# Two-layer hybrid encoder trunk: a room of their own for the gathered rows, one more buffer in the round of weight loads, and a smaller DMA scratch

## The chip, the cores and the metric

The kernel runs on one core of one Trainium2 chip. The metric is the device time of one execution in microseconds (us), shown as the median of several runs. The profile is one further execution, recorded by the hardware profiler; its instruction and DMA times are counted from the start of its span.

## The reference

512 tokens of width 1024 go through two layers and a last RMSNorm, all in float32. A layer is

```
h = rmsnorm(x); p = h @ w_in
o = concat[dilated-window heads | differential heads | latent heads]
x = x + o @ w_out
x = x + expert_choice_ffn(rmsnorm(x))

def expert_choice_ffn(h, ...):            # 16 experts, 64 tokens each
    affinity = softmax(h @ w_router)
    gate, idx = top_k(affinity^T, 64)     # every expert chooses its tokens
    xe = h[idx]                           # gather
    y = (silu(xe @ w_gate) * (xe @ w_up)) @ w_down * gate
    out[idx] += y                         # scatter and add
```

Each expert has three float32 matrices of 1024 x 1408 (w_gate, w_up) and 1408 x 1024 (w_down). All 16 experts of both layers are read once from HBM in each execution, about 554 MB.

## The kernel before, in words

**Phases.** In each layer an attention part (lines to about 880), then the router, which chooses the tokens, and then the expert part (lines 1098 to 1395), which the change is about. The attention part and the expert part use the same addresses of SBUF one after the other: their pools are opened and closed in turn, and a new tile waits until the last reader of whatever lay at its addresses is done.

**Pairs and steps.** The experts are taken two at a time: pair p = 0 to 7, one expert on each half of TensorE's columns. A pair has 24 steps of weights: 8 of the gate matrix, 8 of up, 8 of down. Step n (0 to 191 in a layer) is a block of 128 partitions x 2816 floats (1408 KB). So n = 0 to 7 is gate of pair 0, 8 to 15 up of pair 0, 16 to 23 down of pair 0, 24 to 31 gate of pair 1, 32 to 39 up of pair 1, and so on. Gate and up steps are the matmuls of line 1302, down steps those of line 1347. The order of the matmuls on TensorE is the order of the program.

**Loads.** `load(n)` issues the DMA of step n on the queue of SyncE (SP), in order of n; SP stands still at a load until its buffer is free, and with it everything behind it on that queue. Steps 0 to 16 are issued during the attention part in the order of the list `ISSUE`, each into a buffer as its place in SBUF comes free (line 1131, tiles `xslot`, `shared`, `apart`, `hx`). Steps 17 to 31 take the single buffers a second time in the order of the list `AGAIN` (line 1131, `xslot`). From step 32 on two steps come with one DMA of 2816 KB (line 1163, `dslot`) into one of seven double buffers, in the order of the string `DOUBLES`. Double buffer a lies where the single buffers x0 and x1 were, b where x2 and x3 were, and so on to f (x10, x11); g lies on y0 and y1. The last eight steps are issued one by one again.

**The list before.** With `AGAIN` = x0 to x9, y0, y1, x10, x11, x0, step 17 goes into x0, 18 into x1, ..., 26 into x9, 27 into y0 (free when step 11 is done), 28 into y1 (step 12), 29 into x10 (step 14), 30 into x11 (step 15), and 31 into x0 again (free when step 17 is done). With `DOUBLES` = bcdegfa, the steps 32 and 33 go into b (free when steps 19 and 20 are done), 34 into c (21, 22), 36 into d (23, 24), 38 into e (25, 26), 40 into g (27, 28), 42 into f (29, 30), 44 into a (31, 18).

**Marks and rows.** While pair p runs, pair p + 1 is prepared. At gate step `MARK_AT` = 6, `marks(p + 1)` builds the one-hot marks of the chosen tokens (line 1177), TensorE turns them into token numbers (line 1221) that VectorE copies into `slots` (lines 1225 to 1230), and turns the marks (lines 1236, 1239). `fetch_rows(p + 1)` then gathers the chosen 128 rows of x from HBM with one indirect DMA on GpSimd (POOL) (line 1248, 512 KB), and ScalarE (ACT) scales them (line 1249). After the up steps of pair p, ACT applies Silu to the gate sums (line 1327), VectorE (DVE) multiplies with the up sums (line 1328), `turn_rows` transposes the fetched rows for pair p + 1 (lines 1256, 1257), TensorE transposes the hidden values (line 1336), DVE copies them (line 1337), and the down steps begin (line 1347).

**Where the rows lie.** The rows of pairs 1 to 7 are put into the tile `shared`, tag `rows`, of 3072 floats. In the beginning of a layer's expert part this place holds the weights of step 10 (`(10, "rows")` in `ISSUE`). So the rows of pair 1 are fetched later than those of the others: after up step `ROWS_AT` = 2 of pair 0, which is step 10.

**Scratch.** `dynamic_dma_scratch_size` is the number of bytes of each SBUF partition that are set aside for the descriptors of the DMAs that POOL issues.

Of the kernel before, what the change touches and what calls it, by code (L numbers as in the profile page):

```python
# [11 lines left out]
F32 = mybir.dt.float32  # L12
# [10 lines left out]
P = 128  # L23
S = 512
D = 1024
# [4 lines left out]
FF = 1408  # L30
NJ = FF // P
CAP = 64
SLOT = 3072
RING = 3
ISSUE = [(16, "apart"), (0, "x0"), (1, "x1"), (4, "x4"), (11, "y0"), (2, "x2"), (3, "x3"), (10, "rows"), (5, "x5"), (6, "x6"), (7, "x7"), (9, "x9"), (8, "x8"), (13, "hx"), (14, "x10"), (15, "x11"), (12, "y1")]
AGAIN = ["x0", "x1", "x2", "x3", "x4", "x5", "x6", "x7", "x8", "x9", "y0", "y1", "x10", "x11", "x0"]
SINGLES = 32
DOUBLES = "bcdegfa"
GAP = 512
PAD = 168  # L40
AFTER = [[2, 3, 5, 8], [1, 5, 7, 10], [2, 3, 6, 9]]
# [20 lines left out]
ANGLES_FIRST = 26  # L62
EARLY = [[(0, 1)], [(1, 1)], [(2, 1)], [(3, 1)], []]
HALF_AT = 3
ROWS_AT = 2
END_ON = 'avavaa'
MARK_AT = 6
TAKE_UP = (3, 5)
# [72 lines left out]
def body(ctx, tc, x_in, x_t, pos, w_in, w_uq, w_ukv, w_out, w_gate, w_up, w_down, gatt, gfin, params, consts, band, sel, out):  # L141
    nc = tc.nc
# [7 lines left out]
    def nm(s):  # L150
        uid[0] += 1
        return f"{s}_{uid[0]}"
# [722 lines left out]
    for l in range(L):  # L875
        with ExitStack() as es:
# [218 lines left out]
            both = wide[:, :P].rearrange("p (t c e) -> p t c e", t=NT, c=2)  # L1095
            nc.vector.scalar_tensor_tensor(both, rank, 1.0, mask, op0=ALU.add, op1=ALU.mult)
            nc.vector.tensor_tensor(code, both[:, :, 0, :], both[:, :, 1, :], op=ALU.add)
        with tc.tile_pool(name=f"fs{l}", bufs=1, reuse_waits="tile") as fs, tc.tile_pool(name=f"fw{l}", bufs=2, side="right", reuse_waits="tile") as fw, ExitStack() as late:
            early = ExitStack()
            fx = early.enter_context(tc.tile_pool(name=f"fx{l}", bufs=1, reuse_waits="tile"))  # L1100
            streams = (w_gate, w_up, w_down)
# [1 line left out]
            def wide():  # L1103
                return fw.tile([P, 2 * FF], F32, tag="hx", bufs=1, name=nm("hx"))

            def shared():

                return fs.tile([P, SLOT], F32, tag="rows", name=nm("shared"))

            def single(tag):  # L1110
                return fx.tile([P, 2 * FF], F32, tag=tag, name=nm("xslot"))

            def source(n):

# [16 lines left out]
                    tc.keep_in_program_order(nc.sync.dma_start(v, src))  # L1131
                kept[n] = v

            near = {tag: single(tag) for tag in ("y0", "y1")}
            fx.tile([P, GAP], F32, tag="gap", name=nm("gap"))
            near.update({f"x{i}": single(f"x{i}") for i in range(12)})
            rooms = {}
            for n, tag in ISSUE:
                bring(n, xb.tile([P, 2 * FF], F32, tag="apart", name=nm("apart")) if tag == "apart" else wide() if tag == "hx" else shared()[:, : 2 * FF] if tag == "rows" else near[tag])

            def double(tag):
                return rooms["far"].tile([P, 4 * FF], F32, tag=tag, name=nm("dslot"))
# [1 line left out]
            def load(n):  # L1144

                if n not in kept:
                    if n < SINGLES:
                        bring(n, single(AGAIN[n - len(ISSUE)]))
                    else:
                        if n == SINGLES:  # L1150
                            early.close()
                            rooms["far"] = late.enter_context(tc.tile_pool(name=f"fd{l}", bufs=1, reuse_waits="tile"))
                            rooms["g"] = double("g")
                            rooms["far"].tile([P, GAP], F32, tag="gap", name=nm("gap"))
                            rooms.update({q: double(q) for q in "abcdef"})
                        tag = DOUBLES[(n - SINGLES) // 2 % len(DOUBLES)]
                        v = rooms.pop(tag) if tag in rooms else double(tag)
                        parts = [v[:, i * 2 * FF : (i + 1) * 2 * FF] for i in range(2)]
                        if n >= 23 * KD:
                            for i in range(2):  # L1160
                                bring(n + i, parts[i])
                        else:
                            tc.keep_in_program_order(nc.sync.dma_start(v, source(n)))
                            kept.update({n + i: parts[i] for i in range(2)})
                v = kept.pop(n)
                return v[:, :FF], v[:, FF:]
# [75 lines left out]
            def fetch_rows(p):  # L1242

                if p > 0:
                    v, src = shared()[:, :D], xrow_d[l][:, :]
                else:
                    v, src = fw.tile([P, S], F32R, tag="oh", bufs=3, name=nm("rows")).bitcast(F32), xrow_d[l].rearrange("t (h d) -> (t h) d", h=2)
                nc.gpsimd.indirect_dma_start(v, None, src, bass.IndirectOffsetOnAxis(token[:, p : p + 1], 0))  # L1248
                nc.scalar.activation(v, v, AF.Copy, scale=scales[:, p : p + 1])  # L1249
                return v  # L1250
# [41 lines left out]
            for p in range(8):  # L1292
                acc, whole = [], {}
                ahead = [] if p < 7 else [(t, h) for t in range(NT - 1) for h in range(2)] if l == L - 1 else [(t, h) for h in range(2) for t in range(NT)][:6]
                for s, w in enumerate((w_gate, w_up)):
                    bs = [bank() for _ in cuts]
                    acc.append(bs)
                    for k in range(KD):
                        ws = load((3 * p + s) * KD + k)
                        for b, (q0, qn) in zip(bs, cuts):  # L1300
                            for i in range(2):
                                tc.keep_in_program_order(nc.tensor.matmul(b[64 * i : 64 * i + 64, : qn * NJ], xe[:, k, 64 * i : 64 * i + 64], ws[i][:, q0 * NJ : (q0 + qn) * NJ], start=(k == 0), stop=(k == KD - 1)))  # L1302
                        if ahead and w is w_up and k in TAKE_UP:
                            take_x(*ahead.pop(0))
                        if w is w_gate and p == 0:
                            for f in EARLY[k + 1] if k + 1 < len(EARLY) else ():
                                fill(xg, xe, *f, pin=True)
                            if k == FIRST_MARKS:
                                numbers(first_oh, 0, pin=True)
                                rows = fetch_rows(0)  # L1310
                            if k == TURN_AT:
                                ohs[0] = turn_marks(first_oh, pin=True)
                            if k == HALF_AT:
                                turn_rows(rows, xe, 4, 4)
                        if w is w_gate and k in SCATTER_AT and pending is not None:
                            scatter(*pending, 2 * SCATTER_AT.index(k))
                        if w is w_gate and k == MARK_AT and p < 7:
                            ohs[p + 1] = marks(p + 1)
                            if p > 0:
                                rows = fetch_rows(p + 1)  # L1320
                        if w is w_up and k == ROWS_AT and p == 0:
                            rows = fetch_rows(1)
                hx = wide()
                hh, hT = hx[:, :FF].rearrange("p (j q) -> p j q", j=NJ), hx[:, FF:].rearrange("p (j s) -> p j s", j=NJ)
                for g, u, (q0, qn) in zip(acc[0], acc[1], cuts):
                    hv = hh[:, :, q0 : q0 + qn].rearrange("p j q -> p q j")
                    nc.scalar.activation(hv, g[:, : qn * NJ].rearrange("p (q j) -> p q j", j=NJ), AF.Silu)
                    nc.vector.tensor_tensor(hv, u[:, : qn * NJ].rearrange("p (q j) -> p q j", j=NJ), hv, op=ALU.mult)  # L1328
                if p < 7:
                    nxt = gathered()  # L1330
                    for k0 in (0, 4):
                        turn_rows(rows, nxt, k0)
                for j0, n in ((0, 4), (4, 4), (8, 3)):
                    b = bank()
                    for q in range(n):
                        nc.tensor.transpose(b[:, q * P : (q + 1) * P], hh[:, j0 + q, :], ident)
                    nc.vector.tensor_copy(hT[:, j0 : j0 + n, :], b[:, : n * P].rearrange("p (q s) -> p q s", q=n))
                bs = [bank(), bank()]
                for lo in range(0, NJ * D, FF):
                    hi = lo + FF  # L1340
                    ws = load((3 * p + 2) * KD + lo // FF)
                    e = lo
                    while e < hi:
                        j, h = e // D, e % D // 512
                        z = min(hi, (e // 512 + 1) * 512)
                        for i in range(2):
                            tc.keep_in_program_order(nc.tensor.matmul(bs[h][64 * i : 64 * i + 64, e % 512 : e % 512 + z - e], hT[:, j, 64 * i : 64 * i + 64], ws[i][:, e - lo : z - lo], start=(j == 0), stop=(j == NJ - 1)))  # L1347
                        e = z
                    if ahead and lo > FF:
                        take_x(*ahead.pop(0))  # L1350
                ys = results(p, bs)
                if p < 7:
                    pending = ohs.pop(p), ys
                    xe = nxt
# [133 lines left out]
```

## Time and profile before

| | |
|---|---|
| median of 3 runs | 1909.98 us (1909.73 to 1911.14) |
| the profiled execution's own time | 1910.87 us |
| its span | 1909.1 us |
| PE busy | 1722.2 us (90%), 8798 instructions |
| DVE, ACT, POOL busy | 703.6, 428.6, 206.1 us |
| read from HBM | 619.17 MB |
| DMA queue of SP and its share of 16 engines | 608.43 MB, 78.7% |
| DMAs issued by POOL (software queue) | 35.54 MB, 12128 packets, 7.9% |

The two expert parts are the stretches from about 325 to 950 us and from about 1267 to 1895 us. PE is TensorE's matmuls, PEld its weight loads; a "q" behind an engine's name is its sequencer, where DMAs are issued. PEclk is the granted clock of TensorE as a share of full speed. The time from issue to landing of a DMA holds the time that it spends behind other DMAs.

### The profile page before, as it was taken

The page shows a single profiled execution, that of the slowest core. Times are in us where ns is not written, and L with a number is a line of the kernel's source. Part 1 is how long each engine was busy: PE and PEld are TensorE (multiplying, and loading weights), DVE is VectorE, ACT ScalarE, POOL GpSimd, SP SyncE. Part 2 cuts the span into 40 slices and gives each one's busy share as a digit, 9 for nine tenths or more (in the row PEclk, how much of TensorE's full clock was granted, in tenths as well). Part 3 has the DMA queues.
Part 4 walks back from the last instruction along what each step waited for, and adds up shares of the span by engine and source line. Part 5 has one row for each costly group of instructions (what it writes and reads, how often), then busy time and mean ns, then how long its engine had stood idle before and what let it go on. Part 6 is the DMA issues. An engine that isn't in the chain of part 4 may idle for free.

```text
span 1909.1 us, 21766 instructions
## 1 busy us (share of the span) xinstructions
PE 1722.2 (90%) x8798; PEld 895.9 (47%) x8798; DVE 703.6 (37%) x1470; ACT 428.6 (22%) x884; POOL 206.1 (11%) x232
## 2 busy tenths in 40 slices
PE   8999999999987878888899999989998878888887
PEld 6785675344332333333377756743443333333333
DVE  7868856111211112111188698541121112111112
ACT  5347941101000100000043589211100100000101
POOL 1324421000000000000023153210000000000000
PEclk9999998999999999999999999989999999999999
DMA  7874649989999999999948744798999999999996
GB/s 274 248 199 72 163 149 365 396 351 429 429 428 431 428 430 429 429 428 429 397 131 267 170 101 110 246 363 352 409 429 428 430 429 429 429 429 428 430 427 264
DMA packets 82579, 649.28 MB, mean 340 GB/s; under 512 B 8656, under 2 KB 25808, under 8 KB 53040
## 3 DMA queue, kind: packets, MB, share of 16 engines
q1 hardware_dynamic: 68288, 608.43, 78.7%
q0 software_dynamic: 12128, 35.54, 7.9%
q10 hardware_dynamic: 2064, 3.93, 0.6%
q8 instruction: 69, 1.13, 0.2%
q14 instruction: 30, 0.25, 0.0%
HBM read 619.17 MB, written 27.39 MB: 339 GB/s over the span
## 4 chain that ended last, share of the span: by engine, by line
PE 48%; DMA 37%; DVE 9%; ACT 3%; issue 1%; POOL 1%; SPq 0%; DVEq 0%; ACTq 0%; POOLq 0%
PE ps L1302 16%; DMA dslot<-in_w_up_dram 13%; DMA dslot<-in_w_gate_dram 13%; DMA dslot<-in_w_down_dram 9%; PE ps L1347 7%; PE ps L753 6%; PE ps L854 5%; PE ps L762 2%; PE ps L672 2%; PE ps L1277 2%; PE ps L655 2%; DVE sm L604 1%; PE ps L515 1%; ACT P L611 1%; DMA shared<-xrow_d,slots 1%
## 5 line engine op out<-in xcount | busy, mean ns | idle before, releaser
L1302 PE MATMUL ps<-dslot,xe 128*64 128x506 f32 (+1 forms) x2496 | 528.7, 575 | 87.3 <-DMA dslot<-in_w_up_dram 51.7
L1302 PEld LDWEIGHTS ps<-dslot,xe 128*64 128x64 f32 x2496 | 178.3, 139 | 425.8 <-issue 321.3
L1347 PE MATMUL ps<-dslot,hx 128*64 128x512 f32 (+3 forms) x1568 | 275.8, 504 | 46.1 <-DMA dslot<-in_w_down_dram 41.6
L1347 PEld LDWEIGHTS ps<-dslot,hx 128*64 128x64 f32 x1568 | 104.5, 137 | 209.4 <-issue 136.9
L1328 DVE TENSOR_TENSOR hx<-ps,hx 128x506 f32<-128x506 f32 (+1 forms) x48 | 43.4, 968 | 428.7 <-PE ps L1302 383.7
L1269 DVE SCALAR_TENSOR_TENSOR hx<-ps,gates,hx 128x512 fp32r<-128x512 f32 x32 | 22.5, 746 | 363.3 <-ACT hx L1268 363.3
L1268 ACT ACTIVATE hx<-ps,gates 128x512 fp32r<-128x512 f32 x32 | 20.3, 684 | 605.1 <-PE ps L1347 605.1
L753 PE MATMUL ps<-xh,w 128*128 128x512 f32 (+1 forms) x448 | 145.8, 405 | 3.1 <-ACT xh L363 1.4
L1279 DVE TENSOR_TENSOR x<-ps,x 128x512 f32<-128x512 f32 x112 | 69.5, 683 | 184.1 <-PE ps L1277 184.1
L1249 ACT ACTIVATE shared<-shared,slots 128x1024 f32<-128x1024 f32 x14 | 16.1, 1148 | 488.5 <-DMA shared<-xrow_d,slots 455.3
L611 ACT ACTIVATE P<-ps,sm 128x512 f32<-128x512 f32 x168 | 116.5, 704 | 32.1 <-DVE sm L604 30.8
L1248 POOL DMA_INDIRECT shared<-xrow_d,slots x14 | 13.2, 943 | 945.6 <-DVE oh L1239 887.6
L1302 PE MATMUL ps<-xslot,xe 128*64 128x506 f32 (+1 forms) x528 | 109.4, 560 | 3.9 <-DVE xe L1208 2.3
L753 PEld LDWEIGHTS ps<-xh,w 128*128 128x128 f32 (+1 forms) x448 | 84.2, 189 | 28.0 <-ACT xh L363 3.9
L753 PE MATMUL ps<-xl,w 128*128 128x512 f32 (+1 forms) x224 | 85.7, 393 | 0.0
L604 DVE TENSOR_REDUCE sm<-ps 128x1 f32<-128x512 f32 x120 | 78.7, 679 | 5.5 <-PE ps L589 4.6
L655 PE MATMUL ps<-ident,P 128*128 128x128 f32 x512 | 77.5, 274 | 2.0 <-ACT P L611 1.8
L663 ACT COPY pt<-ps 128x512 f32<-128x512 f32 x118 | 68.9, 604 | 25.9 <-PE ps L655 25.9
L655 PEld LDWEIGHTS ps<-ident,P 128*128 128x128 f32 x512 | 62.1, 140 | 25.6 <-ACT P L611 7.4
L1302 PEld LDWEIGHTS ps<-xslot,xe 128*64 128x64 f32 x528 | 35.8, 136 | 67.4 <-issue 59.6
L762 PE MATMUL ps<-w,xh 128*128 128x320 f32 (+1 forms) x256 | 62.2, 326 | 2.3 <-DVE w L340 2.3
L340 DVE TENSOR_TENSOR w<-slot,w 128x1024 fp32r<-128x1024 f32 (+4 forms) x46 | 53.7, 1170 | 26.3 <-ACT w L339 23.4
(290 smaller groups left out, 2088.6 us busy)
## 6 DMA issues: line engine op xcount, KB each, us to landing
dslot<-in_w_up_dram SPq DMA_DIRECT2D x56, 2816.0 KB, 42.6
dslot<-in_w_down_dram SPq DMA_DIRECT2D x48, 2816.0 KB, 41.0
dslot<-in_w_gate_dram SPq DMA_DIRECT2D x48, 2816.0 KB, 41.8
xslot<-in_w_gate_dram SPq DMA_DIRECT2D x32, 1408.0 KB, 9.5
xslot<-in_w_down_dram SPq DMA_DIRECT2D x14, 1408.0 KB, 9.0
dslot<-in_w_down_dram SPq DMA_DIRECT2D x14, 1408.0 KB, 36.1
xslot<-in_w_up_dram SPq DMA_DIRECT2D x12, 1408.0 KB, 10.0
slot<-in_w_in_dram SPq DMA_DIRECT2D x8, 1536.0 KB, 9.6
```

What stands on the lines that cost most here:

```text
L340: rest = lambda o=o, m=m, src=src: nc.vector.tensor_tensor(w[:, 1, :, o : o + m], src, w[:, 0, :, o : o + m].bitcast(F32), op=ALU.subtract)
L604: nc.vector.tensor_reduce(mn, ps, axis=AX.X, op=ALU.min)
L611: nc.scalar.activation(e, ps, AF.Exp, bias=mn, scale=-1.0, accum_out=lcol)
L655: nc.tensor.transpose(b[:, kc * P : (kc + 1) * P], e[:, kc * P : (kc + 1) * P], ident)
L663: nc.scalar.copy(dv, bv)
L753: nc.tensor.matmul(b[:m], w[:, passes[j][0], k, :m], passes[j][1](k), start=(n == 0), stop=(n == 3 * KD - 1))
L762: nc.tensor.matmul(acc[t][:, :m], xs, w[:, c, kk, :], start=(k == 0 and j == 0), stop=(k == KD - 1 and j == 2))
L854: nc.tensor.matmul(blocks[t][1 + h], o, w[h], start=(i == 0), stop=(i == 3 * KD - 1))
L1279: nc.vector.tensor_tensor(xv, b, xv, op=ALU.add)
L1302: tc.keep_in_program_order(nc.tensor.matmul(b[64 * i : 64 * i + 64, : qn * NJ], xe[:, k, 64 * i : 64 * i + 64], ws[i][:, q0 * NJ : (q0 + q ...
L1328: nc.vector.tensor_tensor(hv, u[:, : qn * NJ].rearrange("p (q j) -> p q j", j=NJ), hv, op=ALU.mult)
L1347: tc.keep_in_program_order(nc.tensor.matmul(bs[h][64 * i : 64 * i + 64, e % 512 : e % 512 + z - e], hT[:, j, 64 * i : 64 * i + 64], ws[i][ ...
```

## The change

The rows of pairs 1 to 7 get a tile of 1024 floats in the pool `xb`, which is open through the whole kernel. The pool `fs` and its tile `shared` are gone. The place of 3072 floats becomes the single buffer `s` of the pool `fx`, with the same position in SBUF as before; step 10 is loaded into it as before, and it takes a second load in the round: `AGAIN` is now x0 to x9, s, y0, y1, x10, x11. `DOUBLES` is now abcdegf. From step 32 on the place of `s` stays empty. The rows of pair 1 are fetched together with its marks at gate step 6 of pair 0, as those of the other pairs are; `ROWS_AT` is gone. The scratch is 1024 bytes instead of 4096.

```diff
-ISSUE = [(16, "apart"), (0, "x0"), ..., (3, "x3"), (10, "rows"), (5, "x5"), ...]
-AGAIN = ["x0", "x1", "x2", "x3", "x4", "x5", "x6", "x7", "x8", "x9", "y0", "y1", "x10", "x11", "x0"]
+ISSUE = [(16, "apart"), (0, "x0"), ..., (3, "x3"), (10, "s"), (5, "x5"), ...]
+AGAIN = ["x0", "x1", "x2", "x3", "x4", "x5", "x6", "x7", "x8", "x9", "s", "y0", "y1", "x10", "x11"]
-DOUBLES = "bcdegfa"
+DOUBLES = "abcdegf"
-ROWS_AT = 2
...
-            def shared():
-                return fs.tile([P, SLOT], F32, tag="rows", name=nm("shared"))
             def single(tag):
-                return fx.tile([P, 2 * FF], F32, tag=tag, name=nm("xslot"))
+                return fx.tile([P, SLOT if tag == "s" else 2 * FF], F32, tag=tag, name=nm("xslot"))[:, : 2 * FF]
...
+            near = {"s": fx.tile([P, SLOT], F32, tag="s", name=nm("slot"))[:, : 2 * FF]}
+            near.update({tag: single(tag) for tag in ("y0", "y1")})
...
+                            rooms["far"].tile([P, SLOT], F32, tag="s", name=nm("lay"))
                             rooms["g"] = double("g")
...
                 if p > 0:
-                    v, src = shared()[:, :D], xrow_d[l][:, :]
+                    v, src = xb.tile([P, D], F32, tag="rows", name=nm("rows")), xrow_d[l][:, :]
...
                             ohs[p + 1] = marks(p + 1)
-                            if p > 0:
-                                rows = fetch_rows(p + 1)
-                        if w is w_up and k == ROWS_AT and p == 0:
-                            rows = fetch_rows(1)
+                            rows = fetch_rows(p + 1)
...
-    nc = _bacc.Bacc("TRN2", ..., dynamic_dma_scratch_size=4096)
+    nc = _bacc.Bacc("TRN2", ..., dynamic_dma_scratch_size=1024)
```

## Rows read from the trace of the kernel before

**Rows 1.** Chain of waits, 900 to 1000 and 1830 to 1910: start us, us, what

```profile
878.65 40.11 DMA dslot<-in_w_up_dram
...
1818.55 43.40 DMA dslot<-in_w_up_dram
```

**Rows 2.** By stretch: length, PE, PEld, DVE, ACT, POOL busy (xcount), PEclk, DMA share, GB/s

```profile
410.00:900.00 490.00, 424.02 (x2185) 170.54 (x2185) 86.92 (x152) 32.04 (x39) 6.22 (x7) 0.99 1.01 429
...
380.00:384.00 4.00, 4.00 (x14) 1.77 (x14) 1.61 (x3) 0.00 (x0) 0.00 (x0) 0.50 0.96 406
384.00:388.00 4.00, 4.00 (x28) 1.63 (x26) 0.00 (x0) 0.00 (x0) 0.00 (x0) 0.94 0.11 44
```

**Rows 3.** Timeline of SP: issues of steps 30, 32, 34; then layer 1's 30, 32

```profile
374.45 0.33 SPq L1131 DMA_DIRECT2D xslot<-in_w_gate_dram  x1
394.86 0.33 SPq L1163 DMA_DIRECT2D dslot<-in_w_up_dram  x1
399.60 0.33 SPq L1163 DMA_DIRECT2D dslot<-in_w_up_dram  x1
...
1316.38 0.33 SPq L1131 DMA_DIRECT2D xslot<-in_w_gate_dram  x1
1337.22 0.33 SPq L1163 DMA_DIRECT2D dslot<-in_w_up_dram  x1
```

**Rows 4.** DMA issues, us to landing: layer 0's 30 and 34, layer 1's 30, 32

```profile
xslot<-in_w_gate_dram SPq DMA_DIRECT2D x1, 1408.0 KB, 11.7
dslot<-in_w_up_dram SPq DMA_DIRECT2D x1, 2816.0 KB, 12.4
...
xslot<-in_w_gate_dram SPq DMA_DIRECT2D x1, 1408.0 KB, 12.4
dslot<-in_w_up_dram SPq DMA_DIRECT2D x1, 2816.0 KB, 9.9
```

**Rows 5.** Chain of waits, layer 0, end of the up steps of pair 0

```profile
362.88 9.30 DMA shared<-xrow_d,slots
...
373.50 1.28 ACT L1327
...
381.17 20.74 PE ps L1347 x112
```

**Rows 6.** Timeline, transposes of the rows at the end of pair 0, layer 0 and layer 1

```profile
374.34 1.10 PE L1256 MATMUL ps<-ident,shared 128*128 128x128 f32 x8
...
1316.27 1.10 PE L1256 MATMUL ps<-ident,shared 128*128 128x128 f32 x8
```

**Rows 7.** End of pair 1's up steps, layer 0: two of the timeline, one of the chain

```profile
444.35 2.72 DVE L1328 TENSOR_TENSOR hx<-ps,hx 128x506 f32<-128x506 f32 x3 [21.66 <-PE ps L1302]
445.68 1.09 PE L1256 MATMUL ps<-ident,shared 128*128 128x128 f32 x8
...
448.92 19.13 PE ps L1347 x112
```

**Rows 8.** Timeline, end of pair 1's marks; and pair 2's fetch, us to landing

```profile
353.02 0.69 DVE L1239 CAST oh<-ps 128x512 fp32r<-128x512 f32 x1
...
shared<-xrow_d,slots POOLq DMA_INDIRECT x1, 13.2
```

**Rows 9.** Timeline, layer boundary: first load of layer 1 on SP; first weight cast on ACT

```profile
931.53 0.34 SPq L322 DMA_DIRECT2D pg<-in_params_dram  x1
...
957.50 1.04 ACT L339 CAST w<-slot 128x1024 fp32r<-128x1024 f32 x1
```

**Rows 10.** POOL's densest DMAs; all of their kind, us to landing; packets of a row fetch

```profile
136.57 2.19 POOL L524 DMA_DIRECT2D st<-bst_d  x4 [21.32 <-PE ps L762]
139.12 2.15 POOL L524 DMA_DIRECT2D st<-bst_d  x4 [0.37 <-PE ps L528]
...
st<-bst_d POOLq DMA_DIRECT2D x40, 256.0 KB, 4.2
q0 software_dynamic: 144, 0.52, 11.8%
```

More of the change, by code (lines that the diff above doesn't have):

```diff
@@ L34 @@
 RING = 3
-ISSUE = [(16, "apart"), (0, "x0"), (1, "x1"), (4, "x4"), (11, "y0"), (2, "x2"), (3, "x3"), (10, "rows"), (5, "x5"), (6, "x6"), (7, "x7"), (9, "x9"), (8, "x8"), (13, "hx"), (14, "x10"), (15, "x11"), (12, "y1")]
-AGAIN = ["x0", "x1", "x2", "x3", "x4", "x5", "x6", "x7", "x8", "x9", "y0", "y1", "x10", "x11", "x0"]
+ISSUE = [(16, "apart"), (0, "x0"), (1, "x1"), (4, "x4"), (11, "y0"), (2, "x2"), (3, "x3"), (10, "s"), (5, "x5"), (6, "x6"), (7, "x7"), (9, "x9"), (8, "x8"), (13, "hx"), (14, "x10"), (15, "x11"), (12, "y1")]
+AGAIN = ["x0", "x1", "x2", "x3", "x4", "x5", "x6", "x7", "x8", "x9", "s", "y0", "y1", "x10", "x11"]
 SINGLES = 32
-DOUBLES = "bcdegfa"
+DOUBLES = "abcdegf"
 GAP = 512
@@ L1097, in body @@
             nc.vector.tensor_tensor(code, both[:, :, 0, :], both[:, :, 1, :], op=ALU.add)
-        with tc.tile_pool(name=f"fs{l}", bufs=1, reuse_waits="tile") as fs, tc.tile_pool(name=f"fw{l}", bufs=2, side="right", reuse_waits="tile") as fw, ExitStack() as late:
+        with tc.tile_pool(name=f"fw{l}", bufs=2, side="right", reuse_waits="tile") as fw, ExitStack() as late:
             early = ExitStack()
@@ L1132, in bring @@
                 kept[n] = v
-            near = {tag: single(tag) for tag in ("y0", "y1")}
+            near = {"s": fx.tile([P, SLOT], F32, tag="s", name=nm("slot"))[:, : 2 * FF]}
+            near.update({tag: single(tag) for tag in ("y0", "y1")})
             fx.tile([P, GAP], F32, tag="gap", name=nm("gap"))
@@ L1138, in body @@
             for n, tag in ISSUE:
-                bring(n, xb.tile([P, 2 * FF], F32, tag="apart", name=nm("apart")) if tag == "apart" else wide() if tag == "hx" else shared()[:, : 2 * FF] if tag == "rows" else near[tag])
+                bring(n, xb.tile([P, 2 * FF], F32, tag="apart", name=nm("apart")) if tag == "apart" else wide() if tag == "hx" else near[tag])
             def double(tag):
@@ L1474 @@
     from concourse.bass_utils import run_bass_kernel_spmd as _run
-    nc = _bacc.Bacc("TRN2", target_bir_lowering=False, num_devices=1, dynamic_dma_scratch_size=4096)
+    nc = _bacc.Bacc("TRN2", target_bir_lowering=False, num_devices=1, dynamic_dma_scratch_size=1024)
     arrays, args = {}, []
```

## The prediction

> **What bounds the kernel now.** I read the page's summary first (TensorE 90% busy, SP's queue 78.7% of the DMA engines), then the chain of waits, then the stretches, then the loads one by one. The reader should see three things.
>
> The expert part of a layer is a stream of weights. From 410 to 900 us the engines moved 429 GB/s at a DMA share of 1.01 [rows 2]: nothing more fits in. By that rate a step of 1408 KB takes 3.36 us and a double one 6.72 us. The last wait in each layer is for a load of the up matrix of pair 7: step 182 lands at 878.65 + 40.11 = 918.8 us, its like in layer 1 at 1818.55 + 43.40 = 1862.0 [rows 1]. Behind these landings stand only the last matmuls and the end of the layer. So a microsecond that the stream loses anywhere after it has filled up is paid at the end of the layer.
>
> It loses some at its beginning. From 384 to 388 us the share is 0.11 [rows 2]. Step 30 landed at 374.45 + 11.7 = 386.15 and step 34 at 399.60 + 12.4 = 412.0 [rows 3, 4]. Between lie 25.9 us, but the loads in them (31, then two doubles) are 3.36 + 2 x 6.72 = 16.8 us of work. **9.1 us** were lost. In layer 1 step 30 landed at 1316.38 + 12.4 = 1328.8 and step 32 at 1337.22 + 9.9 = 1347.1: 18.3 us for 10.1 us of work, **8.2 us** lost.
>
> The reason is in the order of the buffers. Step 31 waits in x0 until step 17 is done, step 32 in b until step 20 is done; both are down steps of pair 0. And these come late, for the rows of pair 1 could be fetched only at 362.88, when step 10 had left their place. They landed at 372.2; ACT then scaled them, loaded its table (1.28 us) and began Silu at 374.8 [rows 5], although TensorE had ended the up steps before 374.34, where it starts to transpose the rows [rows 6]. The down steps began at 381.17, and TensorE's clock had dropped: 0.50 granted from 380 to 384, that is its level of 1.2 GHz [rows 2].
>
> **The change, part by part.**
>
> *Rows with the marks.* The fetch goes out when the marks of pair 1 are done, 353.02 + 0.69 = 353.7 us [rows 8], in place of 362.88. It lands 9.3 us later [rows 5], or 13.2 as for pair 2 [rows 8]: at 363.0 to 366.9. Behind it on ACT wait the scaling (1.15 us), the table and three Silus (2.6); nothing else is due there. All are done at 368 to 372. DVE needs the first Silu where the last up sums end, by pair 1 1.33 us ahead of the rows' transposes (444.35 against 445.68 [rows 7]), so at 373.0. It fits, with 1 us to spare in the worse case. POOL has nothing behind this fetch before pair 2's. The fetch itself is 0.52 MB, 1.2 us of the stream, moved some 9 us ahead within it: the bytes stay the same, and the loads that it then delays are of down steps, which TensorE reaches after 377 us at the earliest, so this costs nothing (were the cover gone: 1.2 us a layer).
>
> Then the end of pair 0 looks like that of pair 1, where the down steps start 448.92 - 445.68 = 3.24 us after the transposes [rows 7]. Pair 0 would start them at 374.34 + 3.24 = 377.6, not 381.17, and run them in 19.13 us, not 20.74 [rows 5, 7], because the long idle time ahead of them is gone: 3.6 + 1.6 = 5.2 us earlier for TensorE at the end of pair 0. In layer 1: 1316.27 + 3.24 = 1319.5 [rows 6].
>
> *The eleventh step's buffer.* Steps 27 to 31 each take the buffer freed one load before, so step 31 is no longer tied to step 17: it may go out when step 15 is done, where step 30 goes out now (374.45), and lands right behind it, 386.15 + 3.36 = 389.5 (layer 1: 1332.1). Step 32 now waits for step 18 in a, not 20 in b. A down step takes 19.13 / 8 = 2.39 us, so step 18 is done at 377.6 + 3 x 2.39 = 384.8 (layer 1: 1326.7). A load into an empty stream has its first bytes after about 9.9 - 6.72 = 3.2 us [rows 4]: 388.0, ahead of 389.5 (layer 1: 1329.9 ahead of 1332.1). The stream does not stop. Step 34 (b, free after step 20 at 389.5) needs to flow at 396.2, 36 (after 22 at 394.3) at 403, and the distance grows by 6.72 - 4.8 us for each double. So both losses go in full: 9.1 + 8.2 = **17.3 us**. Unknown here: whether the gap closes wholly; I take it so, with 0 to 4 us left open, since the margins are 1.5 and 2.2 us.
>
> TensorE does not need these loads at once, and its own 5.2 us are not added: the landing at 918.8 decides, and it moves by the stream's gain. What is late next is again that landing, 9.1 us earlier.
>
> *The names in the round.* The double buffers still come round after seven, so the wait between a load and its buffer is the same from step 46 on. But a and g are each last used one double step later. In layer 1's beginning SP waits for a with its load of `pg` at 931.53 [rows 9], and behind it stand all loads of w_in. Two steps are 4.8 us. The loads queue behind the last weights anyhow, and ACT takes the first of them at 957.50 [rows 9], 26 us later. I take 0, bounds 0 to +4.8, once.
>
> *The scratch.* No row shows a descriptor ring. At its densest POOL issues eight DMAs in 136.57 to 141.27 us [rows 10], and at most seven of these are under way together, as the first lands some 4.2 us after its issue. Bounds: nothing, or one DMA at a time (the last rival). I take nothing, the nearest row: a row fetch has 144 packets, nine on each of 16 engines [rows 10], and so have these; seven are 63. The Trainium skill ("DMA: Bandwidth & Descriptors", "Terms" and "The descriptor swizzle") has descriptors of 16 bytes and nine reads and nine writes an engine for a transfer to 128 partitions, which agrees with the 144; by its "SWDGE vs HWDGE vs iDMA" the rings are in the scratch. As an estimate from that page 1024 bytes hold 64, seven DMAs, and the eighth would wait for the first to land, which it does by then: a few tenths of a us. No run here shows it.
>
> *Addresses.* The rows' 4096 bytes less 3072 of scratch shift the rest by 1024 bytes; no row prices that, I take 0.
>
> **Sum.** The profiled execution took 1910.87 us (span 1909.1): 1910.87 - 17.3 = 1893.6. The median is 0.89 us below that execution, so **1892.7 us**.
>
> **The rivals.**
>
> 1. *The stage doesn't get shorter.* If ACT's table load or the order on DVE holds the down steps where they are, step 18 is done at 394.86 - 2 x 2.39 = 390.1, first bytes come at 393.3 and not 389.5: 3.8 us stay lost, in layer 1 (1337.22 - 4.78 + 3.2 = 1335.6 against 1332.1) 3.5. Gain 17.3 - 7.3 = 10.0: 1900 us. For it: the margin on ACT is thin with the longer landing. Against: pair 1 does the same work behind the same kind of fetch without a gap.
> 2. *The loss is hidden anyway.* TensorE waits for no load until long after 412 us; if the stream found its lost time again, or the end of the layers hung on TensorE, nothing would come of it: 1910 us. For it: TensorE is 90% busy. Against: 429 GB/s throughout, and a landing is what ends last [rows 1, 2].
> 3. *Slower: the small ring makes POOL's DMAs follow one another.* If 1024 bytes let only one be under way, each of the 40 loads of `st` [rows 10] holds POOL for its 4.2 us instead of 0.55. In the burst of eight the last would land after 8 x 4.2 = 33.6 us, where now it lands about 141.27 + 4.2 - 136.57 = 8.9 us after the first issue; the heads behind it start up to 25 us later, in each layer: +50 - 17.3 = +33, 1943 us. It decides from 8.7 us a layer on. For it: the scratch is a quarter. Against: the 63 above. The skill's page named there would have it cost next to nothing.
>
> **How the numbers follow.** Forecast 0.66, the first rival 0.17, the second 0.08, the third 0.05, other things 0.04. The forecast's own range is 1890 to 1897 (0 to 4 us left open, some way below for what the shift may bring). To leave out no more than 2 in 10 the range must take in the first rival: **1888 to 1902**. A measurement tells this kernel from no change at about 0.2%, 3.8 us. Faster by more: 0.66 + 0.17 and a little of the rest, 0.86; within 0.07; slower 0.07.
>
> **What would show it.** In the changed trace: pair 1's fetch on POOL near 354 and its scaling on ACT before 368; the down steps of pair 0 starting 3.2 us after the rows' transposes, at a granted clock of 1.00, in 19.1 us; the load of step 31 right behind step 30, step 32 near 385; a DMA share of 1.0 from 380 to 400; the last up load of layer 0 landing near 909.7, and layer 1's near 1845. The attention part must look as before. It is wrong if the share still dips near 390, if the final landing moves by less than the dip did, or if POOL's DMAs of line 524 become longer or further apart.

## The result, and the profile after

The changed kernel takes **1893.69 us** (median of 4 runs, 1893.06 to 1894.68) against 1910.56 (1909.73 to 1911.46): a ratio of 0.9913, 95% interval 0.9901 to 0.9925. The profiled execution took 1893.34 us, its span 1891.6. The forecast was 1892.7, and its own sum for a profiled execution 1893.6.

The stream first. Four stretches of the changed kernel, in the columns of [rows 2]; lines 1299, 1341 and 1160 of the changed kernel are 1302, 1347 and 1163 of before.

```profile
410.00:890.00 480.00, 412.00 (x2152) 166.53 (x2150) 84.77 (x148) 32.08 (x39) 6.21 (x7) 1.00 1.01 429
380.00:384.00 4.00, 4.00 (x26) 1.64 (x24) 0.00 (x0) 0.00 (x0) 0.00 (x0) 1.00 1.01 421
384.00:388.00 4.00, 4.00 (x26) 1.60 (x24) 0.00 (x0) 0.00 (x0) 0.00 (x0) 1.00 1.07 451
388.00:392.00 4.00, 4.00 (x28) 1.80 (x26) 0.00 (x0) 0.00 (x0) 0.00 (x0) 1.00 1.01 431
```

The hole is gone: from 384 to 388 us the DMA share is 1.07 where it was 0.11, and TensorE's granted clock is 1.00 (2.4 GHz) from 380 on where it was 0.50 [rows 2]. Behind 410 us nothing has changed: the rate is again 429 GB/s.

The issues on SP, layer 0's steps 30, 31, 32 and 34, then layer 1's 30 and 32 (they answer to [rows 3]), and below them, from the view of the DMA issues, what each took to land ([rows 4]):

```profile
371.52 0.33 SPq L1126 DMA_DIRECT2D xslot<-in_w_gate_dram  x1
373.89 0.33 SPq L1126 DMA_DIRECT2D xslot<-in_w_gate_dram  x1
384.37 0.33 SPq L1160 DMA_DIRECT2D dslot<-in_w_up_dram  x1
389.10 0.33 SPq L1160 DMA_DIRECT2D dslot<-in_w_up_dram  x1
...
1304.49 0.33 SPq L1126 DMA_DIRECT2D xslot<-in_w_gate_dram  x1
1317.34 0.33 SPq L1160 DMA_DIRECT2D dslot<-in_w_up_dram  x1
```

```profile
xslot<-in_w_gate_dram SPq DMA_DIRECT2D x1, 1408.0 KB, 14.9
xslot<-in_w_gate_dram SPq DMA_DIRECT2D x1, 1408.0 KB, 16.0
dslot<-in_w_up_dram SPq DMA_DIRECT2D x1, 2816.0 KB, 12.2
dslot<-in_w_up_dram SPq DMA_DIRECT2D x1, 2816.0 KB, 14.2
...
xslot<-in_w_gate_dram SPq DMA_DIRECT2D x1, 1408.0 KB, 14.3
dslot<-in_w_up_dram SPq DMA_DIRECT2D x1, 2816.0 KB, 11.5
```

Adding the two lists line by line: step 30 lands at 386.4, 31 at 389.9, 32 at 396.6, 34 at 403.3. From step 30 to step 34 that is 16.9 us for 16.8 us of work; before it was 25.9. In layer 1, 30 lands at 1318.8 and 32 at 1328.8: 10.0 us instead of 18.3. The longer time to landing is itself a sign of health: before, step 32 of layer 1 landed 9.9 us after its issue, into an empty stream; now it takes 11.5, for it queues behind others.

The end of pair 0's up steps, on ACT and then on TensorE (timelines; rows of before in [rows 5, 6]):

```profile
363.69 1.15 ACT L1246 ACTIVATE rows<-rows,slots 128x1024 f32<-128x1024 f32 x1 [24.27 <-DMA rows<-xrow_d,slots]
364.86 1.28 ACT L1321 ACT_TABLE_LOAD   x1
369.17 2.63 ACT L1321 ACTIVATE hx<-ps 128x506 f32<-128x506 f32 x3 [3.03 <-PE ps L1299]
```

```profile
366.59 2.53 PE L1299 MATMUL ps<-hx,xe 128*64 128x506 f32 x12
368.95 4.90 PE L1299 MATMUL ps<-xslot,xe 128*64 128x506 f32 x24
...
373.78 1.09 PE L1253 MATMUL ps<-ident,rows 128*128 128x128 f32 x8
375.23 1.42 PE L1330 MATMUL ps<-ident,hx 128*128 128x128 f32 x11 [0.35 <-DVE hx L1322]
377.02 1.51 PE L1341 MATMUL ps<-apart,hx 128*64 128x512 f32 x6 [0.37 <-DVE hx L1331]
```

TensorE goes from the rows' transposes (373.78) to the down steps (377.02) in 3.24 us, as for pair 1 in [rows 7]; in before that way took 6.8 us.

The last waits, from the chain of waits of the changed kernel (start, us, what):

```profile
896.67 33.72 DMA dslot<-in_w_down_dram
...
1800.47 43.98 DMA dslot<-in_w_up_dram
```

Layer 1's last up load lands at 1844.45, 17.5 us before that of [rows 1]. In layer 0 the chain now runs through a down load, landing at 930.39; the last up load (step 182, issued at 868.28, 41.8 us to landing) is there at 910.1 instead of 918.8.

### The profile page after: what moved, and what is told of

It is laid out like the page before. It is cut to its first block, busy times and chain, and to the rows that moved or that the text cites. A ratio compares the mean times of both kernels' runs of the same rounds, so it can differ in the third digit from the quotient of the medians.

```text
span 1891.6 us, 21760 instructions
## 1 busy us (share of the span) xinstructions
PE 1706.7 (90%) x8798; PEld 891.8 (47%) x8798; DVE 703.6 (37%) x1470; ACT 428.6 (23%) x884; POOL 205.4 (11%) x232
## 4 chain that ended last, share of the span: by engine, by line
PE 47%; DMA 38%; DVE 9%; ACT 3%; issue 1%; SPq 1%; POOL 1%; DVEq 0%; ACTq 0%; POOLq 0%
PE ps L1299 16%; DMA dslot<-in_w_up_dram 14%; DMA dslot<-in_w_down_dram 13%; DMA dslot<-in_w_gate_dram 11%; PE ps L1341 6%; PE ps L752 6%; PE ps L853 5%; PE ps L761 2%; PE ps L671 2%; PE ps L1274 2%; PE ps L654 2%; DVE sm L603 1%; PE ps L514 1%; ACT P L610 1%; DVE P L638 1%
## 5 line engine op out<-in xcount | busy, mean ns | idle before, releaser
L1299 PE MATMUL ps<-dslot,xe 128*64 128x506 f32 (+1 forms) x2496 | 520.4, 567 | 97.4 <-DMA dslot<-in_w_up_dram 62.1
L1246 ACT ACTIVATE rows<-rows,slots 128x1024 f32<-128x1024 f32 (+1 forms) x16 | 17.5, 1095 | 500.5 <-DMA rows<-xrow_d,slots 486.7
L1245 POOL DMA_INDIRECT rows<-xrow_d,slots x16 | 15.4, 961 | 957.8 <-DVE oh L1236 889.3
L662 ACT COPY pt<-ps 128x512 f32<-128x512 f32 x118 | 68.9, 604 | 26.2 <-PE ps L654 25.8
```

What stands on the lines that cost most here:

```text
L662: nc.scalar.copy(dv, bv)
```

## The experiments

Each run's ratio is against the kernel before, measured beside it: 1910.31 us (median) beside the first four runs, 1911.54 beside the last four, 1910.56 beside the changed kernel. So about 1 us of a difference between the changed kernel and runs 5 to 8 may be no more than that. The table counts landings from the first expert matmul of the layer's stage, as the traces have them, so that the attention part ahead (which moved by a few us between traces of kernels that don't change it) drops out.

| kernel | median us | ratio, 95% | step 32 lands, layer 0 / 1 | step 180 lands, layer 0 / 1 |
|---|---|---|---|---|
| before | 1910.56 | | 77.6 / 78.1 | 585.0 / 585.3 |
| changed | 1893.69 | 0.9913 (0.9901 to 0.9925) | 70.1 / 69.5 | 576.9 / 577.3 |
| 1 rows only | 1902.46 | 0.9962 (0.9947 to 0.9976) | 74.5 / 72.5 | 582.0 / 579.8 |
| 2 fetch a little later | 1895.90 | 0.9926 (0.9913 to 0.9939) | 70.0 / 71.0 | 576.9 / 577.9 |
| 3 scratch only | 1910.54 | 1.0001 (0.9992 to 1.0010) | 77.1 / 77.5 | 584.9 / 584.9 |
| 4 ACT's order only | 1899.90 | 0.9947 (0.9934 to 0.9960) | 72.6 / 73.1 | 579.8 / 580.7 |
| 5 round turned by one | 1900.51 | 0.9941 (0.9927 to 0.9954) | 73.1 / 73.2 | 581.4 / 581.4 |
| 6 round turned by two | 1914.35 | 1.0015 (1.0006 to 1.0025) | 77.4 / 76.8 | 587.2 / 586.2 |
| 7 fetch behind up step 3 | 1901.45 | 0.9950 (0.9936 to 0.9963) | 72.3 / 75.2 | 579.8 / 582.0 |
| 8 fetch behind up step 4 | 1905.83 | 0.9968 (0.9956 to 0.9980) | 74.8 / 76.8 | 582.6 / 583.3 |

Steps 32 and 180 lie 500 us apart, and what a kernel is late at the first it is late at the second, within 1.5 us but for run 6, which loses more on the way. That is the theory (a loss at the beginning of the stream is paid at the end of the layer) in one table.

**Run 1: the rows alone.** The changed kernel with the old round.

```diff
-AGAIN = [..., "x9", "s", "y0", "y1", "x10", "x11"]
-DOUBLES = "abcdegf"
+AGAIN = [..., "x9", "y0", "y1", "x10", "x11", "x0"]
+DOUBLES = "bcdegfa"
```

> The changed kernel with the old lists for the loads (step 31 in x0 again, step 32 in b after step 20; the place s holds step 10 alone). Theory (the two parts attack the same dip of the stream, so their gains overlap): the down steps of pair 0 start near 377 as in the changed kernel; step 31 is issued at 382 and still lands right behind step 30; step 32 is issued when step 20 is done, 389.1 instead of 384.4, and lands 2.3 us late in layer 0 and 3.0 in layer 1: 1893.7 + 5.3 = 1899 us. Rival A (the gain is the rows' alone): 1893.7. Rival B (it is the buffers' alone): 1910.6.

Measured 1902.46 us: 8 us faster than before, 9 slower than the changed kernel. The fetch is early, the down steps follow the transposes, and the hole is smaller but there, as its issue of step 32 and its stretches show:

```profile
392.26 0.33 SPq L1160 DMA_DIRECT2D dslot<-in_w_up_dram  x1
```

```profile
326.00:330.00 4.00, 3.62 (x12) 1.63 (x13) 0.29 (x1) 0.00 (x0) 0.00 (x0) 0.50 0.82 349
...
388.00:392.00 4.00, 4.00 (x22) 1.42 (x20) 0.00 (x0) 0.00 (x0) 0.00 (x0) 1.00 0.67 270
392.00:396.00 4.00, 4.00 (x28) 1.80 (x26) 0.00 (x0) 0.00 (x0) 0.00 (x0) 1.00 0.77 253
```

Step 32 goes out at 392.26 instead of 384.37, and the share is 0.67 and 0.77. In the profiled execution (1902.35 us) the 3.5 us above the expectation lie partly in its start: its first expert steps ran at half clock (0.50 from 326 to 330), which put layer 0's down steps 2.1 us later; layer 1, without that, lands step 180 only 2.5 us behind the changed kernel. The other five executions have no profile, so whether they started alike is open. So the fetch's place is worth about half, two thirds where the stage starts at full clock (5.5 of 8.0 us in layer 1), and the round is needed for the rest.

**Run 2: the round with a later fetch.** Marks and fetch of pair 1 behind the second up step of pair 0.

```diff
-if w is w_gate and k == MARK_AT and p < 7:
+if p < 7 and ((w is w_gate and k == MARK_AT) if p > 0 else (w is w_up and k == 1)):
```

> The changed kernel with pair 1's marks and fetch moved back behind up step 1 of pair 0, so that the fetch goes out near 362 as before the change; lists of the loads as changed. Theory: the down steps of pair 0 start near 381 again with the clock at 0.5 for a while, step 18 is done at 390, step 32 lands 3.3 us late (3.1 in layer 1): 1893.7 + 6.4 = 1900 us, up to 1906 if the fetch lands 13 us after its issue. Rival A (rows alone): 1910.6. Rival B (buffers alone): 1893.7.

A miss: 1895.90 us, no dip in layer 0. The fetch went out at 359.23 instead of 352.98, and ACT began Silu at 371.50 instead of 369.17. That was late by about 1 us: DVE's turn, 1.34 us ahead of the transposes as in the changed kernel, would have been at 371.6; it began at 372.58, behind Silu, and TensorE waited for it:

```profile
371.50 2.62 ACT L1321 ACTIVATE hx<-ps 128x506 f32<-128x506 f32 x3
...
372.94 1.09 PE L1253 MATMUL ps<-ident,rows 128*128 128x128 f32 x8
375.33 1.42 PE L1330 MATMUL ps<-ident,hx 128*128 128x128 f32 x11 [1.29 <-DVE hx L1322]
377.11 2.58 PE L1341 MATMUL ps<-apart,hx 128*64 128x512 f32 x12 [0.37 <-DVE hx L1331]
```

The down steps start 4.17 us behind the transposes (3.24 in the changed kernel), and step 32 is issued 0.9 us later, counted from the first expert matmul. Yet it lands no later (70.0 against 70.1), because steps 30 and 31 are still landing: that is the margin of 1.5 us of the prediction. In layer 1 the down steps were 2.3 us later, which cost step 32 1.5 us and step 180 0.6. So the run did not undo the rows' part; what it shows is that a fetch some 6 us later costs next to nothing, by the room on ACT and the margin of the stream together. Runs 7 and 8 go further.

**Run 3: the scratch alone**, in the kernel before.

```diff
-dynamic_dma_scratch_size=4096)
+dynamic_dma_scratch_size=1024)
```

> The kernel before with a scratch of 1024 bytes and nothing else changed. Theory: POOL's DMA issues of line 524 stay at 0.54 us each and the time is that of before, 1910.6 (within 1 us). Rival (small ring): POOL's issues become longer or further apart, some us to 33 us more.

1910.54 us against 1910.31. POOL's densest DMAs in its timeline, and all of that kind in the view of the issues, stand as in [rows 10]:

```profile
136.35 2.31 POOL L524 DMA_DIRECT2D st<-bst_d  x4 [21.34 <-PE ps L762]
139.28 2.16 POOL L524 DMA_DIRECT2D st<-bst_d  x4 [0.62 <-PE ps L655]
```

```profile
st<-bst_d POOLq DMA_DIRECT2D x40, 256.0 KB, 4.2
```

Four issues in 2.16 to 2.31 us, where serial ones would take 4 x 4.2. The third rival falls. The first of the eight landed at 139.78 us, before the last went out at 140.90, so that at most seven were under way together, as the prediction had it.

**Run 4: ACT's order alone.** In the kernel before, with its late fetch and its round, ACT scales the rows behind the three Silus instead of ahead of them.

```diff
-                nc.scalar.activation(v, v, AF.Copy, scale=scales[:, p : p + 1])
+                if p == 0:
+                    scale_rows(v, p)
...
+                    scale_rows(rows, p + 1)   # behind the Silus, in program order
```

> The kernel before, with the scaling of the fetched rows moved behind the Silus in ACT's program, for all pairs; rows fetched as late as before, into the old place, old lists. Theory (what delayed the down steps is ACT's order: the Silus stood behind a scaling that waited for the rows): Silu runs at 369, when step 13 has left hx, the rows are scaled at 372.3 to 373.5, just ahead of their transposes, the down steps start near 377.5, and the time is that of the early rows with the old lists, 1899 us. Rival (the late landing itself delays the stage): 1910.6.

1899.90 us. Its timeline of ACT, and TensorE's rows' transposes and down steps:

```profile
370.14 2.63 ACT L1331 ACTIVATE hx<-ps 128x506 f32<-128x506 f32 x3 [27.70 <-PE ps L1306]
373.18 1.15 ACT L1254 ACTIVATE shared<-shared,slots 128x1024 f32<-128x1024 f32 x1 [0.41 <-issue]
...
374.75 1.09 PE L1260 MATMUL ps<-ident,shared 128*128 128x128 f32 x8
376.20 1.42 PE L1341 MATMUL ps<-ident,hx 128*128 128x128 f32 x11 [0.36 <-DVE hx L1332]
377.99 1.51 PE L1352 MATMUL ps<-apart,hx 128*64 128x512 f32 x6 [0.37 <-DVE hx L1342]
```

The rows are as late as before, yet the down steps follow their transposes by 3.24 us. What held them was the place of the Silus behind the rows on ACT, as the prediction read it from [rows 5], and not the rows themselves. Two things moved with the order: the Silus and their table load, which ran at 341.15 us, in idle time. By itself the order is worth 10.4 us (1910.31 to 1899.90).

**Runs 5 and 6: the round turned.** The changed kernel, step 32 in the buffer that step 20 leaves (5, the old order of the doubles), or step 22 (6).

```diff
-DOUBLES = "abcdegf"
+DOUBLES = "bcdegfa"    # run 5
+DOUBLES = "cdegfab"    # run 6
```

> The changed kernel with the round of pair 0 turned by one place, so that the load of step 32 takes the buffer that step 20 leaves instead of step 18's; all else as changed. My theory (the loads behind step 30 go out when pair 0's down steps leave their buffers, and what step 32 lands later is lost by the whole stream): step 20 leaves at 389.1 and 1322.1 us, 4.7 us after step 18, a landing takes 9.7 us more, so step 32 lands at 398.8 instead of 396.6 in layer 0 and at 1331.8 instead of 1328.9 in layer 1: +2.2 and +2.9 us, 1898.8. Rival (the order of the round is free, because the stream catches up before the layer's last load): 1893.7.

> The same, turned by two places: step 32 takes the buffer that step 22 leaves. My theory: step 22 leaves at 393.8 and 1326.8 us, so step 32 lands at 403.5 and 1336.5 instead of 396.6 and 1328.9: +7.0 and +7.6 us, 1908.3. Rival (the stream catches up): 1893.7. Between: the loss is less than worked out where the stream has slack of its own behind step 32.

1900.51 and 1914.35 us: in the right order, and both above what was worked out, run 5 by 1.7 us (of which about 1 may be the measurement, as said above), run 6 by 6. Two issues of run 6 on SP (steps 32 and 38), their times to landing from the view of the DMA issues, and one stretch:

```profile
393.85 0.33 SPq L1160 DMA_DIRECT2D dslot<-in_w_up_dram  x1
...
414.78 0.33 SPq L1160 DMA_DIRECT2D dslot<-in_w_up_dram  x1
```

```profile
dslot<-in_w_up_dram SPq DMA_DIRECT2D x1, 2816.0 KB, 9.5
...
dslot<-in_w_up_dram SPq DMA_DIRECT2D x1, 2816.0 KB, 12.5
```

```profile
388.00:392.00 4.00, 4.00 (x29) 1.80 (x26) 0.00 (x0) 0.00 (x0) 0.00 (x0) 1.00 0.04 17
```

Step 32 lands at 403.4, as expected (403.5), behind 4 us with next to no transfer. What the expectation left out comes later in the round: buffer g is not left before 414.8 us. In the changed kernel the sixth double load (step 42, issued at 414.76) takes it, in run 6 the fourth (step 38). That one lands at 427.3, 9.5 us after step 36 for 6.7 of work: 2.8 us more. Counted from the first expert matmul, step 32 is 7.3 us late in layer 0 and step 180 is 10.3 (layer 1: 7.3 and 8.9). In run 5 g is taken by the fifth (415.47), and 3.0 us at step 32 become 4.5 (layer 1: 3.7 and 4.0). So the new order does two things: an early buffer for step 32, and a late turn for the buffer that comes free late. Only the first was in the prediction. Run 5 also differs from run 1 in one thing alone, the second load of `s`: with the fetch early and the old order of the doubles, the eleventh buffer brings step 180 no sooner (581.4 and 581.4 against 582.0 and 579.8), and the intervals of the two ratios overlap. In run 1's layer 1 step 31, still tied to step 17, lands 3.4 us behind step 30 all the same. What `s` buys then is in the lists: step 31 no longer takes x0, so that a can be free for step 32.

**Runs 7 and 8: the fetch later still**, behind the third and the fourth up step of pair 0 (the line of run 2 with `k == 2` and `k == 3`).

> The changed kernel with the marks and the fetch of pair 1 behind the third up step of pair 0 (the run before had them behind the second, and the fetch went out at 359.2). One step later is about 2.4 us: fetch at 361.6, rows at 371.4, scaled at 372.5, Silu done 374 to 376, pair 0's down steps from about 379.8 instead of 377.0, step 18's end and step 32's landing 2.8 us later at 399.4. My theory: the two landings of step 30 and 31 still cover part of it, +2.8 us a layer at most, 1897 to 1899.5. Rival (the fetch has no part in the time once it has room of its own): 1893.7.

> The same behind the fourth up step: fetch at about 364, rows at 373.8, scaled at 374.9, Silu done 377, down steps of pair 0 from about 382.5, 5.5 us later than in the changed kernel, step 32's landing at about 402. My theory: +5.5 us a layer, 1904.5, which is the kernel before with the eleventh buffer added alone or less gain. Rival (no part in the time): 1893.7.

1901.45 and 1905.83 us, a little above both expectations. In run 7's layer 1 the first expert steps ran at half clock (0.50 from 1263 to 1267 us), as in run 1's layer 0, and again TensorE is 2.1 us later from there on; its layer 0 lands step 180 2.9 us behind the changed kernel, near the 2.8 worked out. The chain of run 8 (start, us, what) has the fetch in it:

```profile
364.20 9.53 DMA rows<-xrow_d,slots
...
374.98 1.28 ACT L1321
376.26 0.01 issue
376.27 1.03 ACT hx L1321
...
380.03 2.61 PE ps L1330 x11
382.64 17.74 PE ps L1341 x95
```

and its stretches the hole:

```profile
380.00:384.00 4.00, 3.97 (x15) 2.74 (x17) 3.05 (x5) 0.00 (x0) 0.00 (x0) 0.50 1.00 422
...
388.00:392.00 4.00, 4.00 (x28) 1.76 (x26) 0.00 (x0) 0.00 (x0) 0.00 (x0) 1.00 0.00 0
```

Fetch, table, Silu and transposes now stand one behind the other; the down steps begin at 382.6 and nothing moves from 388 to 392 us. Run 7 is the prediction's first rival made real. Its down steps begin 53.4 us (layer 1, with the 2.1: 56.0) after the layer's first expert matmul, against 54.1 (54.8) in before, about the same, so the stage does not get shorter and only the round is left. The rival was priced at 1900; it measured 1901.45. The parts overlap, as run 1's expectation had it. In the layers that started at full clock step 180 is 5.2 us earlier than in before with the round alone (run 7, layer 0), 5.5 with the fetch alone (run 1, layer 1), and 8.1 and 8.0 with both. By the medians it is 10.1, 7.9 and 16.9 us; the two starts at half clock hide some of the overlap in them.

## Why the prediction was right

- **The bound.** Loads decide, and lost time is not found again: the table shows it over ten kernels. The second rival (hidden anyway) falls with it.
- **ACT's order.** Right, and run 4 shows it alone. One thing was not seen: in the changed kernel the first Silu does not follow the table load, it waits 3.03 us more, until TensorE has done the 12 matmuls that read step 13 from `hx` (366.59 + 2.53 = 369.12), the tile that Silu writes. The prediction had ACT done at 368 to 372; it was done at 371.8. DVE needs only the first Silu: where it waits for one it follows Silu's start by 1.08 us (run 2: 371.50, 372.58), so here it could have begun at 370.25 and began at 372.44, 2.2 us to spare. The bound held, the reason for it was incomplete. With the 3.03 us there were 5.2 us of room on ACT. Counted from the first expert matmul, run 2 scales 6.2 us later and its down steps start 0.9 us later; run 7 scales 8.2 us later, they start 2.9 us later, and 2.9 us is also what step 180 of layer 0 loses. The fetch itself went out at 352.98, not at 353.7: it waits for the token numbers in `slots` and not for the turned marks.
- **The down steps.** 3.24 us behind the transposes, in 19.13 us at a clock of 1.00, as worked out from pair 1.
- **The loads.** Step 32 issued at 384.37 (forecast 384.8), landing of 31 at 389.9 (389.5). The margin of 1.5 us, on which 0 to 4 us were left open, was enough: no gap. The 9.1 and 8.2 us between step 30 and step 34 (32 in layer 1) came back in full (9.0 and 8.3). That the buffer g must not come up early in the round was not in the prediction; the order `abcdegf` has it right, and runs 5 and 6 show what it would have cost.
- **The sum.** 17.3 us were forecast for the profiled execution, 17.5 came, but not all of it from there. From the first expert matmul to the last one the layers are shorter by 8.15 and 7.99 us, 16.1 together; 1.4 us lie in the attention parts, which the change leaves alone. In the profiled executions the first expert matmul of layer 0 starts anywhere from 325.6 to 327.5 us, so those 1.4 are not put down to the change, and that 17.5 came so near to 17.3 is in part luck. In layer 0 step 30 itself landed 0.9 us later after the first expert matmul than in before (60.0 against 59.1). So by the prediction's own sign of being wrong (the final landing moves by less than the dip did) layer 0 falls 0.9 us short: step 180 moved 8.1 us, the dip gave back 9.0. Why is not settled: the other kernels have step 30 at 58.9 to 61.2.
- **The boundary.** Taken at nothing: `pg` went out on SP and ACT took its first cast of layer 1, in two rows of the changed kernel's timeline, at

```profile
928.76 0.34 SPq L321 DMA_DIRECT2D pg<-in_params_dram  x1
...
948.79 1.04 ACT L338 CAST w<-slot 128x1024 fp32r<-128x1024 f32 x1
```

  The cast is 8.7 us earlier than in [rows 9], as much as layer 0's last up landing; `pg` is only 2.8 earlier, as the prediction allowed for (a and g are each last used one double later), and that stayed hidden. The prediction had the up landing as the next last wait. In layer 0 it is a down load and SP's queue behind it instead, at no cost that shows: from the last down matmul of layer 0 to the first expert matmul of layer 1 it is 317.9 us, and was 318.8.
- **The scratch.** Nothing, as taken; run 3 has it within 0.1% of no change. The estimate of a full ring at the eighth transfer is neither shown nor refuted: in run 3's burst the eighth did not meet seven others, and a cost of tenths of a us could not be seen.

What remains: the first four expert steps. In the changed kernel step 12 lands at 330.42 and step 22 at 356.57, 26.2 us for six steps of 3.36 and a little of other transfers; each of these loads waits for a buffer that TensorE leaves. From 330.4 to 356.6 us 359 GB/s were moved, where the full stream has 429: by that an estimated 4 us a layer are still lost there. No run tried to get them back.

## What to carry to other kernels

Where a stream of loads is the bound, look for the first stretch after it fills in which its share falls, ask which buffer the next load waits for, and follow that buffer back to the instruction that frees it: here a scaling of other data, queued ahead of Silu on ACT, emptied the stream 10 us later. Give the load that follows the last free buffers the one that is left first, and go on in the order in which the buffers are left: one that is left late holds up, if its turn comes early, all loads behind it (run 6). Before moving a fetch, find what else its consumer's neighbour waits for: only the part beyond that wait counts.

## What was not expected of the hardware

The matmuls behind the last up landing of layer 1 wait equally long and then run at two speeds. First the changed kernel, then the run with the rows alone (timelines of TensorE):

```profile
1844.49 6.64 PE L1299 MATMUL ps<-dslot,xe 128*64 128x506 f32 x24 [2.75 <-DMA dslot<-in_w_up_dram]
```

```profile
1855.18 4.95 PE L1299 MATMUL ps<-dslot,xe 128*64 128x506 f32 x24 [2.75 <-DMA dslot<-in_w_up_dram]
```

After the same wait of 2.75 us the same 24 matmuls took 6.64 us in the one (granted clock 0.50, that is 1.2 GHz, from 1844.8 to 1848.0) and 4.95 in the other (1.00, 2.4 GHz, from 1852 on). The kernel before had 6.64 as well. All ten kernels wait 2.7 to 2.8 us there; runs 1 and 7 alone keep the full clock throughout. So 1.7 us of the end of a layer depend on whether the clock falls in that wait, and these traces do not tell what decides it. It is also why a comparison of last matmuls would have made run 1's layer 1 look 1.7 us better than its loads were.
